# First weight slab cut to one k-tile and issued from ScalarE, normed input made inside the first projection, last output tile scaled on two engines

## Chip, core and metric

The kernel runs on one core of a Trainium2 chip. The metric is device time in microseconds of one execution. TensorE multiplies matrices, VectorE, ScalarE and GpSimd work on tiles, and SyncE (SP), ScalarE and GpSimd issue transfers (DMAs), each through a queue of its own.

## What is computed

Two residual layers on x (512 tokens x 1024 features, float32), and a final RMSNorm.

```python
u = rms_norm(x, norm_e) @ w_in_e          # even layer
q_c, kv_c, k_r, z_b, glu_a, glu_g, z_a = split(u)      # 384, 256, 32, 4 x 1024
o_b = mla(q_c, kv_c, k_r, ...) * silu(z_b)             # 16 heads of attention
o_a = conformer_conv(glu_a, glu_g, ...) * silu(z_a)    # GLU, conv of width 31, LayerNorm
x = x + concat(o_b, o_a) @ w_out_e
u = rms_norm(x, norm_o) @ w_in_o          # odd layer
z_c, xbc, dt_f, dt_b, g_b, g_c, h_d, z_d = split(u)
o_c = ssd_mixer(z_c, xbc, dt_f, dt_b, ...)             # Mamba-2, two directions
o_d = short_conv(g_b, g_c, h_d, ...) * silu(z_d)
x = x + concat(o_c, o_d) @ w_out_o
return rms_norm(x, final_norm)
```

## The kernel before

The program is unrolled, for one core. Each engine runs its own list of instructions in order. A planner sets these lists when the program is built: it goes by the order in which the program was written, and lets a later instruction go first where it expects an earlier one to be still waiting. Semaphores hold each instruction until its inputs are there.

**Products in three parts.** Every large product is done in float32 quality by splitting each operand into a rounded part (hi) and a residual (lo): hi x hi, lo x hi and hi x lo, three matmuls per k-tile of 128. For a weight slab, ScalarE casts the raw slab to hi (L91) and VectorE or GpSimd subtracts to get lo (L96). For channel slabs of the odd layer (`BY_DMA`) ScalarE writes the negative (L93) and a transfer issued by GpSimd adds the raw slab to it (L94).

**Weights.** `Weights` holds the list of all slabs in the order of use. `_prepare` issues the next slab's transfer on SP's queue and emits its split; `fetch(n)` prepares until n slabs are ready; `next` hands one out and keeps one (three for channel slabs) prepared ahead. There are two landing buffers (w_raw) and three pairs of hi and lo. In the odd layer a counter `i` gives every third channel slab an extra landing buffer and every fourth an extra pair. `i` also deals the residuals of the output projections to VectorE or GpSimd in turn.

**The start.** SP's queue loads the gains ne, then the eight tiles xt[k] (128 features x 512 tokens), with the first three slabs between them (`W.fetch` at k = 1, 4, 7) and a fourth behind them, then the constants kc, the token-major x_t (4 x 512 KB) and small parameters. Each xt[k] is multiplied by the gain and split into xg_hi (ScalarE, L266) and xg_lo (VectorE, L267). From x_t, eight squares on ScalarE (L398) and a chain of small VectorE instructions (`rsqrt`) give r4, the reciprocal root mean square of each token.

**The first projection** (qkv, 672 columns) runs in two halves b of 336 columns. A half takes eight k-tiles of weights in slabs of 2, 3 and 3 (first half) and 3, 3 and 2; in each slab `mm_tm` goes over four token tiles, and for each does the hi products and then the lo products. The first half uses the PSUM banks acc (3) and cv, the second sb and tp; ScalarE empties them with the factor r4 (L406).

**The normed input.** After both halves, `along` (L280) spreads r4 along the tokens into bank cv, and for each k VectorE scales xt[k] (L412), ScalarE casts it to xT_hi (L413), and VectorE or GpSimd subtracts to get xT_lo (L414). These feed all the channel-major products of the even layer (`mm_cm`, L325), first the two GLU tiles.

**The end.** The last projection (oo) runs in two halves of 512 columns. For each token tile t of the second half VectorE adds the residual stream (L1062), ScalarE squares (L287), a chain gives 1/rms, and the two halves are scaled by it and by the gain fg: for t < 3 the first on VectorE (L1072) and the second on ScalarE and GpSimd (L1069, L1070), for the last t both on VectorE. SP issues each store (L1073).

Of the kernel before, what the change touches and what calls it, by code (L numbers as in the profile page):

```python
# [6 lines left out]
F32 = mybir.dt.float32  # L7
# [3 lines left out]
AF = mybir.ActivationFunctionType  # L11
# [4 lines left out]
P = 128  # L16
S = 512
NT = 4
# [52 lines left out]
class Weights:  # L71


    def __init__(self, tc, pool, slabs, ahead, raw_bufs, bufs):
        self.tc, self.pool, self.slabs = tc, pool, slabs
        self.ahead, self.raw_bufs, self.bufs = ahead, raw_bufs, bufs
        self.ready, self.i, self.more = [], 0, pool

    def _prepare(self):
        nc = self.tc.nc  # L80
        key, ap, kt, n = self.slabs[self.i]
        eng = nc.vector if key in EARLY or key in ("oe", "oo") and self.i % 2 else nc.gpsimd
        self.i += 1
        more = key in BY_DMA and self.i % 3 == 0
        raw = (self.more if more else self.pool).tile([P, D], F32, name="w_raw", tag="w_raw",
                                                      bufs=1 if more else self.raw_bufs)[:, :kt * n]
        nc.sync.dma_start(raw, ap)
        more = key in BY_DMA and self.i % 4 == 0
        hi, lo = ((self.more if more else self.pool).tile([P, D], F32R, name=nm, tag=nm, bufs=1 if more else self.bufs)
                  [:, :kt * n] for nm in ("w_hi", "w_lo"))  # L90
        nc.scalar.copy(hi, raw)  # L91
        if key in BY_DMA:
            nc.scalar.mul(lo, raw, -1.0)  # L93
            nc.gpsimd.dma_start(lo, raw, accum_op=ALU.add)  # L94
        else:
            eng.tensor_tensor(lo, raw, hi.bitcast(F32), op=ALU.subtract)  # L96
        v = lambda t: t.rearrange("p (k n) -> p k n", k=kt)
        self.ready.append((key, v(hi), v(lo)))
# [27 lines left out]
def weight_slabs(A):  # L126
# [7 lines left out]

    for b in range(2):
        k0 = 0
        for kt in ((2, 3, 3), (3, 3, 2))[b]:
            out.append(("qkv", A["w_qkv"][b, :, k0:k0 + kt].rearrange("p k n -> p (k n)"), kt, 336))
            k0 += kt
    up = lambda g: out.extend((("uq", A["w_uq"][g][:, :768], 2, 384), ("uq", A["w_uq"][g][:, 768:], 1, 384),  # L140
# [37 lines left out]
def trunk(ctx, tc, A, out, dbg=None):  # L178
# [14 lines left out]
    def page(name, tag, dt=F32):  # L193
        return pg.tile([P, S], dt, name=name, tag=tag, bufs=npage[tag])
# [16 lines left out]
    def four(which):  # L211

        tags = [t for t in banks for _ in range(banks[t])]
        return tags[:4] if which == 0 else tags[4:]


    ne = cp.tile([P, KT], F32, name="ne")
    nc.sync.dma_start(ne, A["ne"])
    warm = cp.tile([P, 1], F32, name="warm")
    V.memset(warm, 0.0)  # L220
    SC.activation(warm, warm, AF.Tanh)
    W = Weights(tc, wp, weight_slabs(A), ahead=1, raw_bufs=2, bufs=3)
    kc = cp.tile([P, NKC], F32, name="kc")
    pc = cp.tile([P, NPC], F32, name="pc")
    rc = cp.tile([P, NRC], F32, name="rc")
# [149 lines left out]
    xg = [], []  # L375
    xt = []
    for k in range(KT):
        if k % 3 == 1:
            W.fetch(1 + k // 3)
        xt.append(page("xt", "att"))  # L380
        nc.sync.dma_start(xt[k], A["xT"][k])
        hi, lo = page("xg_hi", "keep", F32R), page("xg_lo", "keep", F32R)
        split_psum(hi, lo, xt[k], ne[:, k:k + 1])
        xg[0].append(hi)
        xg[1].append(lo)
# [15 lines left out]
    mean_eps(ms, ms, D)  # L401
    rsqrt(r4, ms, NT)
    qkv = [wide("qkv")[:, :672] for _ in range(NT)]
    for b in range(2):
        for t, a in mm_tm("qkv", xg, 3, 336, four(b)):
            SC.activation(qkv[t][:, b * 336:(b + 1) * 336], a[:, :336], AF.Copy, scale=r4[:, t:t + 1])  # L406

    rb = along(r4, "cv")
    xT = [], []
    xh, xl = big("xT_hi"), big("xT_lo")  # L410
    for k in range(KT):
        V.scalar_tensor_tensor(xt[k], xt[k], ne[:, k:k + 1], rb, op0=ALU.mult, op1=ALU.mult)  # L412
        SC.copy(xh[:, k], xt[k])  # L413
        (V if k % 2 else G).tensor_tensor(xl[:, k], xt[k], xh[:, k].bitcast(F32), op=ALU.subtract)  # L414
        xT[0].append(xh[:, k])
        xT[1].append(xl[:, k])
    cos, sin = (kcs(n).rearrange("p (t d) -> p t d", t=4) for n in ("cos", "sin"))

    def rope(dst, src, shape, c, s, name, G=V):
# [639 lines left out]
    for h in range(2):  # L1059
        c = slice(h * S, (h + 1) * S)  # L1060
        for t, a in mm_tm("oo", (oh, ol), 8, 512, four(h), 3 if h else 1, None if h else (6, last_group)):
            V.tensor_tensor(x1[t][:, c], a, x1[t][:, c], op=ALU.add)  # L1062
            halves_square(parts[t], x1[t], h)
            if h:
                r = rstd(part=parts[t])
                for i in range(2):
                    o = slice(i * S, (i + 1) * S)
                    if i and t < NT - 1:
                        SC.activation(x1[t][:, o], x1[t][:, o], AF.Copy, scale=r)  # L1069
                        G.tensor_tensor(x1[t][:, o], x1[t][:, o], fg[:, o], op=ALU.mult)  # L1070
                    else:
                        V.scalar_tensor_tensor(x1[t][:, o], x1[t][:, o], r, fg[:, o], op0=ALU.mult, op1=ALU.mult)  # L1072
                    nc.sync.dma_start(out[t * P:(t + 1) * P, o], x1[t][:, o])  # L1073
# [85 lines left out]
```

## Time and profile before

| | us |
|---|---|
| median of 3 runs | 958.86 (955.78 to 959.15) |
| the profiled execution | 958.48 |
| its span, first to last instruction | 956.7 |
| busy: TensorE, VectorE, ScalarE, GpSimd | 920.2, 696.0, 507.7, 310.1 |

Busy time is a sum over the span; two engines that are busy at once both count. "<-" behind an idle time names what ended it. The granted clock is the share of full speed that TensorE was given. L12 is line 12 of the kernel before.

### The profile page before, as it was taken

To read this page: it belongs to the slowest core of one execution; us is meant where nothing else is said; L and a number is where in the kernel's file an instruction comes from. 1 tells how busy PE (TensorE), PEld (TensorE's weight loads), DVE (VectorE), ACT (ScalarE), POOL (GpSimd) and SP (SyncE) were. 2 spreads that over 40 slices of the span, in tenths; PEclk is the share of its full clock that TensorE was granted. 3 is DMA by queue.
4 is the path that set the end of the run, shared out by engine and by line. 5 is a ranking of instruction groups with operands and counts; after the bars stand their busy time and mean duration, and the time that the engine had idled before them with its cause. 6 is when DMAs were issued, how large, how long until landed. Compare 5 with 4: busy or idle time off the path is not lost.

```text
span 956.7 us, 12593 instructions
## 1 busy us (share of the span) xinstructions
PE 920.2 (96%) x4528; PEld 741.1 (77%) x4528; DVE 696.0 (73%) x1292; ACT 507.7 (53%) x964; POOL 310.1 (32%) x269
## 2 busy tenths in 40 slices
PE   7899998999999999999999899999999999999996
PEld 7888686776877677888889578878786886888885
DVE  4699888999988999893163779777866886466315
ACT  6645454544554444373135487777667757444322
POOL 0142716347073443283222121121212222234222
PEclk9999999999999999999999899999999999999998
DMA  8303302212122215423347679868676776732222
GB/s 317 106 28 112 57 22 95 60 51 86 45 70 83 66 56 97 132 92 111 96 161 201 158 211 220 195 157 214 163 196 159 215 170 161 196 113 74 88 81 88
DMA packets 48373, 119.57 MB, mean 125 GB/s; under 512 B 12808, under 2 KB 14472, under 8 KB 48312
## 3 DMA queue, kind: packets, MB, share of 16 engines
q1 hardware_dynamic: 35304, 82.61, 26.7%
q0 software_dynamic: 6480, 23.60, 13.7%
q10 hardware_dynamic: 6528, 12.58, 4.4%
q8 instruction: 35, 0.57, 0.2%
q14 instruction: 26, 0.21, 0.1%
HBM read 90.85 MB, written 4.33 MB: 99 GB/s over the span
## 4 chain that ended last, share of the span: by engine, by line
PE 79%; DVE 13%; DMA 3%; ACT 3%; issue 1%; POOL 0%; SPq 0%; DVEq 0%; ACTq 0%; POOLq 0%
PE acc L325 39%; PE acc L352 10%; PE tp L352 5%; PE sb L352 5%; PE sb L536 5%; PE tp L273 5%; PE acc L573 3%; PE cv L352 3%; PE cv L945 2%; PE tp L961 1%; DMA sums_d<-sums 1%; ACT w_hi L91 1%; PE sb L273 1%; DVE w_lo L96 1%; DMA w_raw<-in_w_cm_o 1%
## 5 line engine op out<-in xcount | busy, mean ns | idle before, releaser
L325 PE MATMUL acc<-xT_hi,w_hi 128*128 128x512 f32 x616 | 249.2, 406 | 2.7 <-ACT xT_hi L413 2.7
L325 PE MATMUL acc<-xT_lo,w_hi 128*128 128x512 f32 x616 | 246.7, 401 | 0.1
L91 ACT CAST w_hi<-w_raw 128x1024 fp32r<-128x1024 f32 (+7 forms) x139 | 134.8, 971 | 200.8 <-PE acc L325 85.6
L325 PE MATMUL acc<-xT_hi,w_lo 128*128 128x512 f32 x616 | 155.1, 391 | 0.0
L96 DVE TENSOR_TENSOR w_lo<-w_raw,w_hi 128x1024 fp32r<-128x1024 f32 (+6 forms) x74 | 83.0, 1121 | 88.2 <-ACT w_hi L91 77.6
L325 PEld LDWEIGHTS acc<-xT_hi,w_hi 128*128 128x128 f32 x616 | 116.9, 190 | 27.3 <-ACT xT_hi L413 2.9
L488 DVE SCALAR_TENSOR_TENSOR cv<-u,pc,cv 128x497 f32<-128x497 f32 (+10 forms) x176 | 130.2, 740 | 10.1 <-ACT cv L477 7.7
L325 PEld LDWEIGHTS acc<-xT_lo,w_hi 128*128 128x128 f32 x616 | 116.8, 190 | 24.5 <-POOL xT_lo L414 0.8
L325 PEld LDWEIGHTS acc<-xT_hi,w_lo 128*128 128x128 f32 x616 | 115.4, 188 | 24.1
L94 POOL DMA_DIRECT2D w_lo<-w_raw x45 | 39.2, 871 | 180.5 <-ACT w_lo L93 128.2
L96 POOL TENSOR_TENSOR w_lo<-w_raw,w_hi 128x1024 fp32r<-128x1024 f32 (+1 forms) x20 | 47.7, 2387 | 112.0 <-ACT w_hi L91 104.2
L486 POOL TENSOR_TENSOR side<-side 128x510 f32<-128x510 f32 (+3 forms) x56 | 78.6, 1403 | 4.7
L491 POOL TENSOR_TENSOR u<-cs,side 128x512 f32<-128x512 f32 x8 | 11.0, 1375 | 157.1 <-issue 149.9
L540 ACT ACTIVATE p<-sb,mx 128x512 f32<-128x512 f32 x64 | 43.4, 683 | 20.8 <-DVE mx L538 20.5
L485 POOL TENSOR_SCALAR side<-u,pc 128x510 f32<-128x510 f32 (+3 forms) x56 | 50.2, 897 | 4.7
L93 ACT ACTIVATE w_lo<-w_raw 128x1024 fp32r<-128x1024 f32 x45 | 47.5, 1056 | 2.2 <-PE acc L325 2.2
L928 DVE SCALAR_TENSOR_TENSOR e<-e,nacs 128x128 f32<-128x128 f32 x96 | 30.1, 347 | 22.6 <-ACT e L927 22.5
L538 DVE TENSOR_REDUCE mx<-sb 128x1 f32<-128x512 f32 x64 | 41.7, 685 | 3.2 <-PE sb L536 2.6
L923 DVE SCALAR_TENSOR_TENSOR f<-cbm,dt,f 128x128 f32<-128x128 f32 x96 | 39.2, 444 | 5.6 <-ACT f L922 5.6
L273 PEld LDWEIGHTS tp<-kc,p 128*128 128x128 f32 x256 | 28.9, 140 | 16.1 <-ACT pt L563 10.7
L728 DVE SCALAR_TENSOR_TENSOR c<-acc,pc,c 128x510 f32<-128x510 f32 (+1 forms) x48 | 35.8, 745 | 6.3 <-ACT c L726 5.7
L536 PE MATMUL sb<-k_t,qk_hi 128*128 128x512 f32 (+1 forms) x128 | 39.5, 403 | 0.4 <-DVE k_t L264 0.4
(325 smaller groups left out, 1836.8 us busy)
## 6 DMA issues: line engine op xcount, KB each, us to landing
w_raw<-in_w_cm_o SPq DMA_DIRECT2D x45, 512.0 KB, 4.8
w_lo<-w_raw POOLq DMA_DIRECT2D x45, 512.0 KB, 5.9
w_raw<-in_w_cm_e SPq DMA_DIRECT2D x32, 512.0 KB, 3.5
e<-acs ACTq DMA_DIRECT2D x24, 512.0 KB, 6.0
w_raw<-in_w_out_e SPq DMA_DIRECT2D x16, 512.0 KB, 3.5
w_raw<-in_w_out_o SPq DMA_DIRECT2D x16, 512.0 KB, 3.3
xt<-in_xT SPq DMA_DIRECT2D x8, 256.0 KB, 5.1
x_t<-in_x SPq DMA_DIRECT2D x4, 512.0 KB, 6.3
```

Of the source, the lines that this page charges most:

```text
L91: nc.scalar.copy(hi, raw)
L93: nc.scalar.mul(lo, raw, -1.0)
L96: eng.tensor_tensor(lo, raw, hi.bitcast(F32), op=ALU.subtract)
L273: T.transpose(tp[:rows, j * P:(j + 1) * P], b, ident)
L325: T.matmul(a, l, r, start=n == 0, stop=n == 3 * kk - 1)
L352: T.matmul(accs[t][:, :n], l, r, start=k1 == 0 and c == 0, stop=end and c == len(seq) - 1)
L485: G.tensor_scalar(t[:, o], ut[:, i], wt(j), 0.0, op0=ALU.mult, op1=ALU.add)
L486: G.tensor_tensor(side[:, o], side[:, o], t[:, o], op=ALU.add)
L488: V.scalar_tensor_tensor(c[:, o], ut[:, i], wt(j), c[:, o], op0=ALU.mult, op1=ALU.add)
L536: T.matmul(s, l[:, qs], r, start=n == 0, stop=n == 2)
L538: V.tensor_reduce(mx, s, axis=AX.X, op=ALU.max, negate=True)
L540: SC.activation(p, s, AF.Exp, bias=mx, accum_out=sums[:, q:q + 1])
```

## The change

The first half's slabs become 1, 2, 3 and 2 k-tiles, one slab more. The first one's transfer is issued by ScalarE ahead of everything (`W.load`), and `_prepare` then takes it over. On SP's queue xt[0] goes first and ne second; slabs are fetched at k = 1, 3 and 5 in place of 1, 4 and 7. The making of the normed input becomes a function, `normed`, which `mm_tm` calls in the second half between its first and its second slab. In the last projection the first 512 columns of the last token tile are multiplied by fg on GpSimd in the first half, and at the end ScalarE scales them and issues their store.

```diff
+    def load(self):
+        _, ap, kt, n = self.slabs[0]
+        self.first = self.pool.tile([P, D], F32, name="w_raw", tag="w_raw", bufs=self.raw_bufs)[:, :kt * n]
+        self.tc.nc.scalar.dma_start(self.first, ap)
     def _prepare(self):
...
-        nc.sync.dma_start(raw, ap)
+        if self.first is not None:
+            raw, self.first = self.first, None
+        else:
+            raw = (self.more if more else self.pool).tile([P, D], F32, name="w_raw", tag="w_raw",
+                                                          bufs=1 if more else self.raw_bufs)[:, :kt * n]
+            nc.sync.dma_start(raw, ap)
...
-        for kt in ((2, 3, 3), (3, 3, 2))[b]:
+        for kt in ((1, 2, 3, 2), (3, 3, 2))[b]:
...
     ne = cp.tile([P, KT], F32, name="ne")
-    nc.sync.dma_start(ne, A["ne"])
+    W = Weights(tc, wp, weight_slabs(A), ahead=1, raw_bufs=2, bufs=3)
+    W.load()
...
-        if k % 3 == 1:
-            W.fetch(1 + k // 3)
+        if k in (1, 3, 5):
+            W.fetch(1 + k // 2)
         xt.append(page("xt", "att"))
         nc.sync.dma_start(xt[k], A["xT"][k])
+        if k == 0:
+            nc.sync.dma_start(ne, A["ne"])
...
-    for b in range(2):
-        for t, a in mm_tm("qkv", xg, 3, 336, four(b)):
-            SC.activation(qkv[t][:, b * 336:(b + 1) * 336], a[:, :336], AF.Copy, scale=r4[:, t:t + 1])
-
-    rb = along(r4, "cv")
     xT = [], []
     xh, xl = big("xT_hi"), big("xT_lo")
-    for k in range(KT):
-        V.scalar_tensor_tensor(xt[k], xt[k], ne[:, k:k + 1], rb, op0=ALU.mult, op1=ALU.mult)
-        SC.copy(xh[:, k], xt[k])
-        (V if k % 2 else G).tensor_tensor(xl[:, k], xt[k], xh[:, k].bitcast(F32), op=ALU.subtract)
-        xT[0].append(xh[:, k])
-        xT[1].append(xl[:, k])
+
+    def normed():
+
+        rb = along(r4, "cv")
+        for k in range(KT):
+            V.scalar_tensor_tensor(xt[k], xt[k], ne[:, k:k + 1], rb, op0=ALU.mult, op1=ALU.mult)
+            SC.copy(xh[:, k], xt[k])
+            (V if k % 2 else G).tensor_tensor(xl[:, k], xt[k], xh[:, k].bitcast(F32), op=ALU.subtract)
+            xT[0].append(xh[:, k])
+            xT[1].append(xl[:, k])
+
+    for b in range(2):
+        for t, a in mm_tm("qkv", xg, 4 - b, 336, four(b), 1, (1, normed) if b else None):
+            SC.activation(qkv[t][:, b * 336:(b + 1) * 336], a[:, :336], AF.Copy, scale=r4[:, t:t + 1])
...
             halves_square(parts[t], x1[t], h)
+            if h == 0 and t == NT - 1:
+                G.tensor_tensor(x1[t][:, c], x1[t][:, c], fg[:, c], op=ALU.mult)
             if h:
                 r = rstd(part=parts[t])
                 for i in range(2):
                     o = slice(i * S, (i + 1) * S)
+                    if t == NT - 1 and i == 0:
+                        SC.activation(x1[t][:, o], x1[t][:, o], AF.Copy, scale=r)
+                        nc.scalar.dma_start(out[t * P:(t + 1) * P, o], x1[t][:, o])
+                        continue
```

## Rows read from the trace of the kernel before

**Rows 1.** The page's busy times (us, share of the span, instructions), and from the list of TensorE's waits over the whole span: who waited for whom, us in total, how often, the longest.

```profile
PE 920.2 (96%) x4528; PEld 741.1 (77%) x4528; DVE 696.0 (73%) x1292; ACT 507.7 (53%) x964; POOL 310.1 (32%) x269
...
PE acc L352 <- ACT w_hi L91: 6.0, 1, 6.0
...
PE acc L325 <- ACT xT_hi L413: 2.7, 1, 2.7
```

**Rows 2.** Windows of 2 us: stretch, its length, busy us and instructions of TensorE, its weight loads, VectorE, ScalarE and GpSimd, then granted clock, share of the DMA engines, GB/s.

```profile
4.00:6.00 2.00, 0.05 (x1) 0.05 (x1) 0.82 (x2) 1.47 (x2) 0.00 (x0) 1.00 0.96 324
...
40.00:42.00 2.00, 0.00 (x0) 0.00 (x0) 2.00 (x3) 1.94 (x8) 0.00 (x0) 1.00 0.03 12
42.00:44.00 2.00, 1.40 (x4) 0.64 (x4) 2.00 (x4) 2.00 (x6) 1.32 (x2) 0.74 0.61 197
44.00:46.00 2.00, 2.00 (x5) 1.61 (x6) 2.00 (x4) 1.73 (x6) 1.72 (x2) 0.50 0.00 0
```

**Rows 3.** The timeline of the first 11 us: start, us, engine, line, instruction. SPq is an issue on SP's queue.

```profile
1.18 0.42 SPq L381 DMA_DIRECT2D xt<-in_xT  x1
...
4.04 0.72 ACT L266 ACTIVATE xg_hi<-xt,ne 128x512 fp32r<-128x512 f32 x1 [1.81 <-DMA xt<-in_xT]
...
5.15 0.75 ACT L91 CAST w_hi<-w_raw 128x672 fp32r<-128x672 f32 x1 [0.38 <-DMA w_raw<-in_w_qkv]
5.93 0.86 DVE L96 TENSOR_TENSOR w_lo<-w_raw,w_hi 128x672 fp32r<-128x672 f32 x1 [0.39 <-ACT w_hi L91]
...
5.95 0.65 PE L352 MATMUL acc<-w_hi,xg_hi 128*128 128x336 f32 x1 [5.95 <-ACT w_hi L91]
...
7.08 0.93 PE L352 MATMUL acc<-w_hi,xg_hi 128*128 128x336 f32 x2 [0.20 <-ACT xg_hi L266]
...
10.33 0.48 PE L352 MATMUL acc<-w_hi,xg_lo 128*128 128x336 f32 x1
...
10.61 0.48 PE L352 MATMUL acc<-w_hi,xg_hi 128*128 128x336 f32 x1
```

**Rows 4.** The timeline of ScalarE, VectorE and TensorE between 15 and 27 us: cast of the second half's first slab, the first square, cast of its second slab; start of the rsqrt chain and the residual behind it; the first two matmuls of the second half (bank sb).

```profile
15.11 1.04 ACT L91 CAST w_hi<-w_raw 128x1008 fp32r<-128x1008 f32 x1 [1.16 <-DMA w_raw<-in_w_qkv]
17.46 0.63 ACT L398 ACTIVATE junk<-x_t 128x512 bf16<-128x512 f32 x1 [1.32 <-DMA x_t<-in_x]
...
23.61 1.03 ACT L91 CAST w_hi<-w_raw 128x1008 fp32r<-128x1008 f32 x1
...
23.51 0.16 DVE L400 TENSOR_TENSOR ss<-ss 128x4 f32<-128x4 f32 x1 [6.12 <-ACT junk L398]
...
25.62 1.21 DVE L96 TENSOR_TENSOR w_lo<-w_raw,w_hi 128x1008 fp32r<-128x1008 f32 x1
...
23.97 0.31 PE L352 MATMUL sb<-w_hi,xg_hi 128*128 128x336 f32 x1
24.12 0.31 PE L352 MATMUL sb<-w_hi,xg_lo 128*128 128x336 f32 x1
```

**Rows 5.** The timeline of TensorE and VectorE between 38 and 49 us: the broadcast of r4, the first GLU matmuls and the ones from which their pace is even; VectorE's first scalings and its last subtraction.

```profile
38.75 1.05 PE L280 MATMUL cv<-kc,r 128*128 128x128 f32 x8
42.50 1.28 PE L325 MATMUL acc<-xT_hi,w_hi 128*128 128x512 f32 x3 [2.70 <-ACT xT_hi L413]
...
46.50 0.39 PE L325 MATMUL acc<-xT_lo,w_hi 128*128 128x512 f32 x1
46.73 0.39 PE L325 MATMUL acc<-xT_hi,w_hi 128*128 128x512 f32 x1
...
40.98 2.72 DVE L412 SCALAR_TENSOR_TENSOR xt<-xt,ne,cv 128x512 f32<-128x512 f32 x4
...
47.97 0.68 DVE L414 TENSOR_TENSOR xT_lo<-xt,xT_hi 128x512 fp32r<-128x512 f32 x1
```

**Rows 6.** The timeline of the end: a scaling on ScalarE of the third tile, the two on VectorE of the last, and their stores on SP's queue.

```profile
948.00 0.73 ACT L1069 ACTIVATE x<-x,rstd 128x512 f32<-128x512 f32 x1 [1.92 <-DVE rstd L255]
...
952.05 1.42 DVE L1072 SCALAR_TENSOR_TENSOR x<-x,rstd,gain 128x512 f32<-128x512 f32 x2
952.83 0.99 SPq L1073 DMA_DIRECT2D out<-x  x2
```

**Rows 7.** The start of the odd layer, in the timeline: GpSimd's issue of the first channel slab's accumulate, ScalarE's cast of a later slab and the exponential of the dt chain, TensorE's transpose of that chain's result. Then the page's transfers: line, queue, number, size, median us from issue to landing.

```profile
511.35 1.04 POOL L94 DMA_DIRECT2D w_lo<-w_raw  x1 [1.52 <-issue]
...
522.12 1.05 ACT L91 CAST w_hi<-w_raw 128x1024 fp32r<-128x1024 f32 x1 [3.86 <-DMA w_raw<-in_w_cm_o]
...
524.41 0.35 ACT L804 ACTIVATE d<-d 128x192 f32<-128x192 f32 x1
...
533.73 0.60 PE L273 MATMUL tp<-kc,d 128*24 128x128 f32 x4 [4.30 <-DVE d L817]
...
w_raw<-in_w_cm_o SPq DMA_DIRECT2D x45, 512.0 KB, 4.8
w_lo<-w_raw POOLq DMA_DIRECT2D x45, 512.0 KB, 5.9
w_raw<-in_w_cm_e SPq DMA_DIRECT2D x32, 512.0 KB, 3.5
```

**Rows 8.** The timeline where the even layer's output projection reaches the Conformer's operands: VectorE's residuals of the second and third of them, and TensorE's first matmul on the first.

```profile
422.17 4.23 DVE L368 TENSOR_TENSOR o_lo<-oT,o_hi 128x512 fp32r<-128x512 f32 x2
...
429.61 0.39 PE L352 MATMUL acc<-w_hi,o_hi 128*128 128x512 f32 x1
```

More of the change, by code (lines that the diff above doesn't have):

```diff
@@ L77, in __init__ @@
         self.ready, self.i, self.more = [], 0, pool
+        self.first = None
+    def load(self):
+        _, ap, kt, n = self.slabs[0]
+        self.first = self.pool.tile([P, D], F32, name="w_raw", tag="w_raw", bufs=self.raw_bufs)[:, :kt * n]
+        self.tc.nc.scalar.dma_start(self.first, ap)
     def _prepare(self):
@@ L84, in _prepare @@
         more = key in BY_DMA and self.i % 3 == 0
-        raw = (self.more if more else self.pool).tile([P, D], F32, name="w_raw", tag="w_raw",
-                                                      bufs=1 if more else self.raw_bufs)[:, :kt * n]
-        nc.sync.dma_start(raw, ap)
+        if self.first is not None:
[4 more added lines that the diff above has]
+            nc.sync.dma_start(raw, ap)
         more = key in BY_DMA and self.i % 4 == 0
@@ L221, in trunk @@
     SC.activation(warm, warm, AF.Tanh)
-    W = Weights(tc, wp, weight_slabs(A), ahead=1, raw_bufs=2, bufs=3)
     kc = cp.tile([P, NKC], F32, name="kc")
```

## Prediction

> **What bounds the kernel now.** I read the shares first: TensorE is busy for 96% of the span, VectorE for 73% [rows 1]. What TensorE waits for is therefore what a change can win, and the list of its waits is short: 6.0 us before the first matmul and one wait of 2.7 us on the cast of the normed input (xT_hi, L413) head it [rows 1]. Then the windows around that second wait: no matmul in 40 to 42 us, and after it a granted clock of 0.74, then 0.50 of full speed (the 1.2 GHz level) until some 46 us [rows 2]. So the wait costs more than its 2.7 us. Next the timeline of the start [rows 3], of the middle of the first projection [rows 4] and of its end [rows 5], then the last microseconds [rows 6] and the stage where the odd layer begins [rows 7]. All sums are made against the profiled execution, 958.48 us (span 956.7 and 1.8 around it), which is 0.4 us below the median of 958.86.
>
> **The start: smaller first slab, other queue, other order.** Before, TensorE starts at 5.95 us, when the cast of the 672-wide slab ends; it issues two matmuls and goes on at 7.08, at 0.28 us each (10.33 to 10.61) [rows 3]; that is the 1.2 GHz level for 336 columns, though the granted clock reads 1.00 there [rows 2]. xt[0] is used 2.86 us after its issue (1.18 to 4.04). Now it is issued where ne stood, 0.44 us earlier, beside a 168 KB slab, so it should be there at 3.6 to 4.0; ne, now behind it in SP's queue, is small and lands with it. ScalarE then needs 0.72 for xg_hi and 0.47 for the 336-wide cast (0.75 for 672 and 1.03 for 1008 [rows 3, 4], 0.28 less per k-tile), and the first matmul comes at 4.8 to 5.2; the residual (0.86 for 672, 1.21 for 1008, so 0.51) lets it run on from about 5.9. At 8.7 us twelve matmuls are done in place of eight: a lead of 4 x 0.28 = 1.1 us. It is between 0.6 (same four at 0.15, if the clock rises no earlier) and 1.5.
>
> The DMA engines are 0.96 busy between 4 and 6 us [rows 2], so a second issuing queue finds little room. The Trainium skill says why this speaks against the queue ("DMA: Bandwidth & Descriptors", "Issuing engines are not separate DMA queues"): transfers issued by different engines run on the same 16 DMA engines, and another issuer saves only the time of issuing. By that rule the queue itself is worth one SP issue, 0.42 us [rows 3], and the best case for the start below would be 0.4 and not 1.0, the sum staying as it is.
>
> **Where that lead goes.** The first fetch prepares four slabs. Before, these hold 2+3+3+3 k-tiles, so the fourth is already the first slab of the second half; its cast runs from 15.11 us, long before TensorE needs it at 23.97 [rows 4]. Now they hold 1+2+3+2, all of the first half. The second half's first slab is fetched only when the loop reaches the last slab of the first, behind kc, x, pc and rc on SP; its cast stands behind the eight squares on ScalarE and its residual behind the rsqrt chain on VectorE, just as the next slab's did before (cast at 23.61 after the squares, residual at 25.62 after the chain [rows 4]). Three k-tiles fewer ahead of x_t are 0.5 MB, 1.5 us at 324 GB/s [rows 2]; with the 0.4 of the earlier start the squares begin at 15.6 instead of 17.46 and take 6.05 (17.46 to 23.51), so they end at 21.6. The cast then ends at 22.7, the chain (2.1) at 23.75, the residual at 24.95. TensorE wants that residual after six matmuls of the first token tile. Before, that was at 23.97 + 6 x 0.15 = 24.9. It is no earlier now: **the lead of 1.1 us is waited away, and I count 0** for the start. Bounds: +1.0 if the residual is put ahead of the chain (22.7 + 1.2 = 23.9), -1.9 if x lands no earlier than before.
>
> **normed() inside the second half.** Moved: four broadcast matmuls (1.05 us for eight instructions), eight VectorE scalings, eight ScalarE casts, four subtractions each on VectorE and GpSimd; nothing is added, and no DMA moves with it. Before, TensorE ends the broadcast at 39.80, idles to 42.50, and starts nine matmuls by 46 us and the tenth by 46.50, where the 0.23 us pace begins [rows 2, 5]. Ten at 0.23 take 2.3 of these 4.0 us. The loss is 2.70 + 1.7 = **4.4 us**. Now the broadcast stands behind the second half's first slab, at 29.6; it needs r4 (23.75) and the cv bank (emptied by about 26), so it does not wait. VectorE's twelve instructions took from 40.98 to 48.65, 7.7 us, and would run from 30.7 to 38.4, GpSimd's four beside them. TensorE still has 60 matmuls of 0.154 us (9.2 us) and reaches the first GLU product at 39.8, where the broadcast ended before, and goes on at full pace. The cover is these 9.2 us; without it the 4.4 are paid as before. Queued behind VectorE's twelve are the later weight residuals: that of the first GLU slab is wanted only 16 x 0.23 = 3.7 us after 39.8, which leaves time.
>
> The one that could be late is the last qkv slab. Its landing buffer is freed at 24.95; a 512 KB slab takes 3.5 to 4.8 us to land [rows 7], its cast 0.75, so its residual can start at 29.2 to 30.5, just ahead of the twelve (30.7). I take that it does.
>
> **The tail.** The last tile's two scalings take 1.42 us on VectorE, and SP issues the two stores from 952.83 to 953.82, 0.33 each [rows 6]. The second scaling and store go to ScalarE (0.73 for the same shape), so both stores are issued at about 952.83: **0.65 us** saved (0 if ScalarE's store is slow to issue, 0.99 at most). The GpSimd product that replaces its gain runs some 40 us earlier and is waited for by nobody.
>
> **The shifted slab count.** One slab more shifts the counter that deals out VectorE or GpSimd residuals for the output projections, and, in the odd layer, which slab gets the extra landing buffer (every third) or extra pair (every fourth). At the odd layer's start ScalarE waits 3.86 us for a slab (cast at 522.12); the exponential of the dt chain is queued behind it (524.41), and TensorE waits 4.30 us for that chain (533.73) [rows 7]. That slab's buffer is held until the accumulate issued at 511.35 has landed (5.9 us: 517.2, and 4.8 more give 522). With the shift the first C slab has the extra pair and need not wait for TensorE to free one. GpSimd idled for 1.52 us before that issue, so it can come **1.5 us** earlier, and the chain with it. Bounds: 0, and all of the 4.3.
>
> **Sum.** 0 + 4.4 + 0.65 + 1.5 = 6.55; 958.5 - 6.55 = 952.0 us. TensorE has work for 96% of the span, so what it saves early should reach the end. The bounds give 947.5 (4.3 at the odd layer, 1.0 at the start, 0.99 in the tail, and 0.3 less if only nine matmuls were started by 46.5) to 955.4 (-1.9 at the start, 0 for the shift).
>
> **Rivals.**
> *The last qkv slab is late.* If its residual falls behind the twelve, it ends at 38.4 + 0.9 = 39.3, while TensorE wants it at 30.7 + 5.5 + 0.6 = 36.8: 2.5 us of the 4.4 return, and without the odd layer's 1.5 that is 956. For it: the margin is 0.2 to 1.5 us. Against: VectorE takes what is ready, and nothing else is at 30.
> *The gain is caught later.* VectorE is the second busiest; the Conformer's operands leave it at 426.40, and TensorE takes them at 429.61 [rows 8], 3.2 us of slack against 4.4 of gain. If VectorE came no earlier, this and its like in the eight head pairs could leave the tail alone: 957.8. Against: VectorE's twelve move into time in which it idled, so it is earlier too.
> *Slower: the extra landing buffer at the wrong slabs.* A slab holds its buffer for 4.8 + 1.05 + 1.05 + 5.9 = 12.8 us; two buffers carry one per 6.4 us, TensorE eats one per 24 x 0.23 = 5.5. Each channel slab whose run of five has lost its third buffer costs 0.9 us. The kernel gets slower by 0.5% from some eleven such slabs of the 45 (5.05 + 4.8 = 9.9 us); fourteen give 966. For it: ScalarE's 3.86 us wait is of this kind. Against: the waits of TensorE name no channel slab.
>
> **How the numbers follow.** Half a per cent, 4.8 us, is what a measurement of this kernel tells from no change. The forecast has 0.62, of which 0.58 lie beyond 4.8 us; the late slab 0.14 and the gain caught later 0.12, both within; the wrong buffers 0.12, of which 0.09 are slower. The range 947.5 to 957.8 leaves out the slower case and a small part below.
>
> **What would show it.** First matmul near 5.0 us; a wait of about 1 us on w_lo near 24; the broadcast near 30 us; no wait on L413 and a granted clock of 1.00 through 40 to 48; the first GLU matmul near 39.8 but at 0.23 us; the last stores issued together 0.65 us earlier. Wrong it would be by a wait on the last qkv residual near 37 us, on the Conformer's operands near 425, or on w_hi or w_lo in the odd layer.

## The result and the profile after

The changed kernel takes 961.56 us (median of 10 runs, 957.37 to 969.88) beside 958.68 us (10 runs) of the kernel before: ratio 1.0043, 95% interval 1.0024 to 1.0062. The ratio is worked out from all runs; the two medians alone lie 2.9 us apart. The changed kernel is thus 2 to 6 us slower, at the middle of the interval 4.1 us, which is less than the half per cent set as the bound of a change. The forecast was 952.0 us with 947.5 to 957.8 as its range: wrong, and on the other side. Two executions of the experiments, 1139.35 us at a granted clock of 0.85 (e8_both) and 1531.18 us at 0.557 (e11_order), are left out of every comparison. The profiled execution after took 964.18 us, span 962.4, against 958.48 and 956.7 [rows 1].

The page's busy line and the list of TensorE's waits after:

```profile
PE 922.1 (96%) x4528; PEld 742.1 (77%) x4528; DVE 702.8 (73%) x1292; ACT 508.0 (53%) x966; POOL 311.9 (32%) x270
...
PE acc L362 <- ACT xg_hi L276: 5.4, 1, 5.4
...
PE tp L283 <- DVE d L832: 2.9, 1, 2.9
PE tp L283 <- DVE qkv L456: 2.4, 1, 2.4
...
PE sb L290 <- DVE rs L265: 2.1, 1, 2.1
...
PE sb L362 <- ACT w_hi L101: 1.2, 1, 1.2
PE sb L362 <- DVE w_lo L106: 0.8, 1, 0.8
```

The wait of 2.7 us on xT_hi is gone, as forecast, and the wait on d (4.3 before [rows 7]) is shorter. But four waits are new: on w_hi and w_lo of a qkv slab, on qkv, and on rs of the LayerNorm. The timeline shows the first two, and what became of the broadcast and of the first GLU product:

```profile
17.54 0.63 ACT L410 ACTIVATE junk<-x_t 128x512 bf16<-128x512 f32 x1 [2.54 <-DMA x_t<-in_x]
...
23.53 1.03 ACT L101 CAST w_hi<-w_raw 128x1008 fp32r<-128x1008 f32 x1
24.62 0.42 PE L362 MATMUL sb<-w_hi,xg_hi 128*128 128x336 f32 x1 [1.19 <-ACT w_hi L101]
25.68 1.21 DVE L106 TENSOR_TENSOR w_lo<-w_raw,w_hi 128x1008 fp32r<-128x1008 f32 x1
26.94 0.73 PE L362 MATMUL sb<-w_lo,xg_hi 128*128 128x336 f32 x3 [0.82 <-DVE w_lo L106]
...
31.36 1.05 PE L290 MATMUL cv<-kc,r 128*128 128x128 f32 x8
41.47 0.40 PE L335 MATMUL acc<-xT_hi,w_hi 128*128 128x512 f32 x1
...
49.07 1.30 PE L283 MATMUL tp<-kc,qkv 128*128 128x128 f32 x5 [2.40 <-DVE qkv L456]
```

The squares start no earlier than before (17.46 [rows 4]), so the second half's first slab is late, and TensorE waits 2.0 us for it (1.19 for its cast, 0.82 for its residual). Windows around the GLU products answer to [rows 2]:

```profile
40.00:42.00 2.00, 2.00 (x14) 1.91 (x13) 2.00 (x3) 2.00 (x5) 1.35 (x1) 1.00 0.00 0
42.00:44.00 2.00, 2.00 (x10) 1.63 (x9) 2.00 (x3) 1.97 (x7) 0.33 (x1) 1.00 0.00 0
44.00:46.00 2.00, 2.00 (x10) 1.67 (x9) 2.00 (x12) 1.91 (x7) 0.00 (x0) 1.00 0.70 238
46.00:48.00 2.00, 0.67 (x3) 0.21 (x2) 1.93 (x19) 1.32 (x4) 0.00 (x0) 1.00 0.63 203
48.00:50.00 2.00, 0.93 (x5) 0.96 (x6) 1.90 (x9) 1.53 (x5) 0.00 (x0) 0.70 0.21 84
50.00:52.00 2.00, 2.00 (x8) 1.71 (x7) 1.24 (x3) 1.12 (x3) 0.00 (x0) 0.50 0.03 8
```

The granted clock is 1.00 where it was 0.50 before, but a hole opens behind it: TensorE works for only 1.60 of the 4 us from 46 to 50, and the clock is 0.50 in 50 to 52 us. The new wait on rs, at 406 us, is the next large loss:

```profile
403.87 0.17 DVE L264 TENSOR_SCALAR rs_t<-rs_t 128x4 f32<-128x4 f32 x1
403.92 2.34 POOL L106 TENSOR_TENSOR w_lo<-w_raw,w_hi 128x1024 fp32r<-128x1024 f32 x1 [13.47 <-PE acc L335]
404.07 2.21 DVE L265 TENSOR_TENSOR rs<-rs_t,rs_w 128x4 f32<-128x4 f32 x1
...
406.33 1.55 PE L290 MATMUL sb<-kc,rs 128*128 128x128 f32 x9 [2.10 <-DVE rs L265]
```

An instruction of 4 columns takes 2.21 us instead of 0.16: it ends when GpSimd ends the subtraction of a weight residual that the shifted count dealt to it (406.28 and 406.26). A low clock follows. Windows of 20 us of the kernel before, then of the changed one:

```profile
400.00:420.00 20.00, 19.96 (x96) 16.67 (x96) 18.66 (x26) 13.34 (x19) 10.49 (x7) 1.00 0.21 65
```

```profile
400.00:420.00 20.00, 17.90 (x83) 14.79 (x83) 17.16 (x34) 9.97 (x14) 6.00 (x4) 0.91 0.15 53
```

**Where each kernel stands.** The table is worked out from the traces: the time of the n-th matmul in the kernel before, and how much later (+) or earlier (-) it starts in the others, in us. Columns: start (75), second half of qkv (175), GLU (200 to 400, at 210 behind the ten matmuls that were slow before), head pairs (1100, 1300), LayerNorm (1900 to 2000), start of the odd layer (2500 to 2600), odd layer to its end.

```
n               75    175    200    210    300    400   1100   1300   1900   2000   2500   2600   3100   3300   4500
before        20.7   36.1   42.5   46.7   64.6   83.1  229.5  270.8  395.1  415.1  522.7  552.0  654.5  693.8  942.1
after         -0.7   +1.5   -1.0   -2.9   +1.5   +1.1   +1.6   +3.1   +3.6   +7.2   +7.2   +4.3   +5.0   +5.7   +5.6
e1_tail       -0.9   -0.9   -0.9   -0.6   +0.2   +0.2   -0.2   -0.6   -0.7   -0.7   -0.7   +1.4   +1.4   +0.2   +0.3
e2_normed     -0.7   -1.0   -3.6   -5.5   -3.3   -4.0   -4.7   -2.1   -3.3   -3.3   -3.3   -1.6   -1.6   -2.7   -2.5
e3_start      -1.0   +0.7   +0.7   +0.5   +1.2   +1.2   -0.6   -0.8   -0.3   +3.2   +3.2   +1.9   +2.7   +5.3   +5.2
e4_deal       -0.8   +1.0   -1.6   -3.5   +1.3   +0.9   +0.2   +1.3   +1.3   +1.3   +1.3   +2.5   +2.5   +3.0   +3.1
e5_early      -1.1   -1.4   -4.0   -5.9   -3.2   -2.3   -1.8   -2.2   -0.6   -0.7   -0.7   +1.3   +1.3   +0.0   +0.3
e6_slabs      -0.0   -0.4   -2.9   -4.9   -2.3   -3.0   -3.3   -1.4   -2.0   -2.0   -2.0   -0.6   -0.6   +0.3   +0.9
e7_parity     -1.4   +0.0   -2.5   -4.4   +0.2   -0.3   -1.5   -0.5   -0.6   -0.6   -0.6   +2.2   +2.8   +4.6   +4.6
e8_both       -0.1   -0.4   -2.9   -4.9   -2.6   -3.5   -3.0   -0.1   +0.0   +0.1   +0.0   -1.1   -0.3   +2.0   +2.5
e9_order      -0.3   -0.6   -3.1   -5.1   -3.2   -3.9   -2.9   -0.7   -0.5   -0.5   -0.5   -1.1   -1.1   -0.5   -0.5
e10_order     -1.2   -1.5   -4.1   -6.0   -3.9   -4.5   -4.5   -2.2   -3.0   -3.0   -3.0   -2.1   -2.0   -3.2   -3.2
e11_order     -1.0   +1.2   -1.4   -3.3   -0.5   -1.2   -1.3   +0.5   +1.1   +4.6   +4.6   +0.2   +0.9   +1.2   +1.2
e12_light     -1.0   -1.0   -1.0   -2.1   -1.4   -1.3   +5.3   +7.5   +8.5   +8.6   +8.6  +10.6  +10.6   +9.6  +10.2
e13_light     -1.0   -1.4   -3.9   -5.8   -3.6   -3.5   +1.3   +2.9   +4.1   +4.1   +4.1   +5.0   +4.9   +3.7   +4.0
```

It has to be read with care: the row e1_tail is a kernel with the same instructions as before up to the tail, and yet it stands 0.9 us earlier at 75 and 2.1 us are lost at the odd layer's start. So a single execution tells some 1 us at the start and 2 us at the odd layer; the comparison of many runs decides there. Nor does a traced execution lie at its kernel's median: 964.18 us beside 961.56 (after), 963.16 beside 959.57 (e7_parity), 959.79 beside 964.95 (e11_order). What the traces repeat is firmer. The 3.5 to 3.6 us between 1900 and 2000 matmuls are lost in all three kernels that keep the shifted dealing (after, e3_start, e11_order), and no more than 0.1 in the eleven others.

### The profile page after: what moved, and what is told of

It reads as the page before. It is cut to its first block, busy times and chain, and to the rows that moved or that the text cites. A ratio compares the mean times of both kernels' runs of the same rounds, so it can differ in the third digit from the quotient of the medians.

```text
span 962.4 us, 12609 instructions
## 1 busy us (share of the span) xinstructions
PE 922.1 (96%) x4528; PEld 742.1 (77%) x4528; DVE 702.8 (73%) x1292; ACT 508.0 (53%) x966; POOL 311.9 (32%) x270
## 4 chain that ended last, share of the span: by engine, by line
PE 70%; DVE 15%; DMA 5%; ACT 4%; issue 4%; POOL 1%; SPq 0%; ACTq 0%; POOLq 0%; DVEq 0%
PE acc L335 35%; PE acc L362 7%; PE tp L283 5%; PE sb L362 4%; PE tp L362 4%; PE sb L551 4%; PE acc L588 3%; PE cv L362 2%; DVE cv L503 2%; DVE w_lo L106 2%; PE cv L960 2%; DMA w_raw<-in_w_cm_e 2%; PE tp L976 1%; ACT w_hi L101 1%; PE sb L283 1%
## 5 line engine op out<-in xcount | busy, mean ns | idle before, releaser
L106 DVE TENSOR_TENSOR w_lo<-w_raw,w_hi 128x1024 fp32r<-128x1024 f32 (+7 forms) x75 | 90.3, 1204 | 82.1 <-ACT w_hi L101 73.3
L501 POOL TENSOR_TENSOR side<-side 128x510 f32<-128x510 f32 (+3 forms) x56 | 75.5, 1349 | 4.7
L938 DVE SCALAR_TENSOR_TENSOR f<-cbm,dt,f 128x128 f32<-128x128 f32 x96 | 41.4, 468 | 5.6 <-ACT f L937 5.6
L588 PE MATMUL acc<-pt,v_tm 128*64 128x512 f32 x128 | 38.4, 608 | 1.8 <-DVE pt L578 1.8
```

What stands on the lines that cost most here:

```text
L501: G.tensor_tensor(side[:, o], side[:, o], t[:, o], op=ALU.add)
L588: T.matmul(o[j * HD:(j + 1) * HD], v_tm[:, k, (h0 + j) * HD:(h0 + j + 1) * HD], pt, start=k == 0, stop=k == NT - 1, skip_group_check=True)
```

## The experiments

**The tail alone (e1_tail).** The kernel before with

```diff
+            if h == 0 and t == NT - 1:
+                G.tensor_tensor(x1[t][:, c], x1[t][:, c], fg[:, c], op=ALU.mult)
...
+                    if t == NT - 1 and i == 0:
+                        SC.activation(x1[t][:, o], x1[t][:, o], AF.Copy, scale=r)
+                        nc.scalar.dma_start(out[t * P:(t + 1) * P, o], x1[t][:, o])
+                        continue
```

> The kernel before with the tail's part of the change alone: the last tile's first half scaled and stored by ScalarE, its gain on GpSimd earlier. Theory A (the forecast's step): both last stores are issued at the time of the first, and the kernel is 0.65 us faster. Theory B (after the profile of the changed kernel): both stores are issued together but share the same DMA engines, so that they land about 0.8 us later after their issue than before (2.85 against 2.06 us), and from the last 1/rms to the end nothing is won: within 0.3 us of the kernel before.

Measured: ratio 1.0000 (0.9983 to 1.0017). The last 1/rms and the two last stores of this run:

```profile
952.13 0.16 DVE L255 TENSOR_TENSOR rstd<-rs_t,rs_w 128x1 f32<-128x1 f32 x1
953.07 0.40 ACTq L1072 DMA_DIRECT2D out<-x  x1
953.10 0.33 SPq L1079 DMA_DIRECT2D out<-x  x1
```

From the start of that instruction to the end of the span (957.0) it is 4.87 us, before 4.84 (951.86 to 956.7 [rows 6]). Both stores are issued within 0.03 us of each other, as forecast, and nothing is won. In the changed kernel the store issued by ScalarE lands 2.85 us after its issue, where the last one before took 2.06. The trace of the kernel before shows why nothing could be won: between 954.0 and 955.0 us its DMA engines show a busy share of 1.02 and 1.03, so the two stores, issued 0.33 us each from 952.83 on, already fill them. With both issued together the share is 1.00 and 1.02 between 954.0 and 955.0. The Trainium skill ("DMA: Bandwidth & Descriptors", "Issuing engines are not separate DMA queues") says that transfers run on the same 16 DMA engines whichever engine issues them, and that a second issuer saves only the time of issuing; the trace agrees. Theory B.

**normed() alone (e2_normed).** The kernel before, with the broadcast, scalings, casts and subtractions in a function that the second half calls:

```diff
+        for t, a in mm_tm("qkv", xg, 3, 336, four(b), 1, (1, normed) if b else None):
```

> The kernel before with normed() inside the second half alone; first slab, queues, slab count and tail as before. Theory A (the forecast's step): TensorE meets the GLU products at the full clock and with no wait on L413's counterpart, and 4.4 us are kept to the end: ratio near 0.9955. Theory B: the wait on the normed input goes, but TensorE then meets the transposes of qkv before VectorE and ScalarE have delivered qkv, waits some 2.4 us there and loses the clock behind it, so that no more than 1 us is kept: ratio 0.999 to 1.001.

Measured: 0.9989 (0.9968 to 1.0010), 1.1 us with an interval of 2 on either side. At the 210th matmul the lead is 5.5 us, 4.4 more than at the 192nd (1.1): the forecast's step is there in full, as it is in the changed kernel (from +1.5 to -2.9). Some 15 matmuls later TensorE waits at the transposes of qkv:

```profile
46.55 1.01 PE L273 MATMUL tp<-kc,qkv 128*128 128x128 f32 x6 [1.75 <-ACT junk L440]
```

That is 1.75 us of the 4.4; the granted clock stayed at 1.00 here. A lead of 3.3 to 4.7 us remains up to 1100 matmuls. Another 2.6 go between 1100 and 1300, and 1.7 at the odd layer's start, which is no more than e1_tail lost there with the old instructions. Theory B, with the later loss still open.

**The start alone, with the shifted count (e3_start).** The changed kernel with

```diff
-        for t, a in mm_tm("qkv", xg, 4 - b, 336, four(b), 1, (1, normed) if b else None):
+        for t, a in mm_tm("qkv", xg, 4 - b, 336, four(b)):
```

the normed input behind the projection and the tail as before.

> The kernel before with the start alone (four slabs of 1, 2, 3, 2 k-tiles, ScalarE's queue, new order on SP), and with it the slab count shifted by one; the normed input made after the projection, the tail as before. Theory A (the forecast): 0 for the start, 1.5 us won at the odd layer, ratio near 0.998. Theory B: x_t lands no earlier, the second half's first slab is late by about 2 us, the LayerNorm's small chain on VectorE is held by GpSimd's residual of an output-projection slab (3.5 us), and the odd layer's start gives back 2.9: 2 to 3 us slower, ratio near 1.0025.

Measured: 1.0055 (1.0031 to 1.0079), 5 us slower, more than expected. The late slab (+1.7 from 75 to 175), the wait on rs (+3.5 from 1900 to 2000) and the gain at the odd layer's start (-1.3) are all there; a wait of 2.0 us on c (L742) near 686 us with a granted clock of 0.91 in 680 to 700 adds 2.6.

**The count brought back (e4_deal).** In the changed kernel:

```diff
-        eng = nc.vector if key in EARLY or key in ("oe", "oo") and self.i % 2 else nc.gpsimd
+        eng = nc.vector if key in EARLY or key in ("oe", "oo") and (self.i - 1) % 2 else nc.gpsimd
...
-        more = key in BY_DMA and self.i % 3 == 0
+        more = key in BY_DMA and (self.i - 1) % 3 == 0
```

and the same for `% 4`.

> The changed kernel, with the count that deals out the residuals and the extra buffers brought back by one, so that every slab behind the first projection is treated as in the kernel before. Theory A (the forecast: the shift is worth 1.5 us): slower than the changed kernel by 1.5 us or more, ratio to the kernel before near 1.006. Theory B: the LayerNorm's small chain near 404 us is undisturbed again (3.5 us won), while the wait on d at the odd layer's start is back at 4.3 us (2.9 lost): about the changed kernel's time, ratio 1.002 to 1.005, with TensorE's wait on rs near 406 gone.

Measured: 1.0019 (1.0001 to 1.0037), faster than the changed kernel by 0.24% or 2.3 us, with an interval of 2.5 on either side. The wait on rs is gone, the wait on d is back at 4.7 us. Theory A's ratio of 1.006 lies outside the interval: the shift of the count, which I had counted as a gain, is none. Theory B. That it costs isn't clear of the noise in this pair of kernels alone.

**The second half's first slab early (e5_early).** The kernel of e4_deal with

```diff
-    W.fetch(4)
+    W.fetch(5)
```

> As the run that brought the count back by one, but five slabs are fetched ahead of kc and x_t in place of four, so that the second half's first slab is cast before the squares, as in the kernel before. Theory A (the late slab costs what TensorE waits at it near 24 us, and by pushing everything behind it also makes VectorE late for the transposes of qkv): no wait on w_hi or w_lo at 24 to 27 us, the lead of 0.7 us kept up to 125 matmuls, and with the wait on qkv gone or shorter the kernel is 2 to 4.5 us faster than that run: ratio to the kernel before 0.997 to 1.000. Theory B (the wait on qkv near 49 us is due to the order of the work alone): the 2 us come back at the transposes, ratio near 1.002 as without it.

Measured: 0.9990 (0.9971 to 1.0010), 2.8 us faster than e4_deal, with an interval of 2.6 on either side. The cast of that slab (first line; the second line is the next slab's) now stands ahead of the squares, which begin at 17.54:

```profile
16.33 1.04 ACT L101 CAST w_hi<-w_raw 128x1008 fp32r<-128x1008 f32 x1 [2.18 <-DMA w_raw<-in_w_qkv]
...
24.98 1.04 ACT L101 CAST w_hi<-w_raw 128x1008 fp32r<-128x1008 f32 x1 [1.43 <-DVE rs_w L262]
```

No wait on w_hi or w_lo is left (from 75 to 175 matmuls -0.3 instead of +1.8), and the longest wait on qkv is 1.4 us instead of 2.4. Theory A.

**Three slabs again (e6_slabs).** The changed kernel with

```diff
-        for kt in ((1, 2, 3, 2), (3, 3, 2))[b]:
+        for kt in ((2, 3, 3), (3, 3, 2))[b]:
...
-        for t, a in mm_tm("qkv", xg, 4 - b, 336, four(b), 1, (1, normed) if b else None):
+        for t, a in mm_tm("qkv", xg, 3, 336, four(b), 1, (1, normed) if b else None):
```

> The changed kernel with the first half in three slabs of 2, 3 and 3 k-tiles again: ScalarE still issues the first one, xt[0] still goes ahead of ne, normed() and the tail stay. So the slab count is that of the kernel before, and the fourth fetch is the second half's first slab. Theory A (what went wrong at the start is the fourth slab of the first half): no wait near 24 us, no wait on rs near 406, and the time of normed() alone or a little less: ratio 0.996 to 0.999. Theory B (ScalarE's queue and the new order delay x_t by themselves): the squares end later than 23.5 us and the ratio stays at 1.002 or more.

Measured: 0.9979 (0.9959 to 0.9998), the lowest ratio of all, though e2_normed and e5_early lie within its interval: 2 us ahead of the kernel before and 6 ahead of the changed one, with intervals of 1.9 and 2.6. No wait on w_hi, w_lo or rs is left. Theory A: the fourth slab of the first half was the fault. It brings both the late slab and the shifted count, and this run doesn't part the two; e5_early, with four slabs, is no slower than the kernel before. With the old 672-wide slab, issued from ScalarE, TensorE starts at 6.29 us, no earlier than before (5.95 [rows 3], and 5.75 to 6.41 in the other traces of the old start): the queue and the new order on SP won nothing together.

**The parity alone (e7_parity).** The changed kernel, with only the first of the three lines of e4_deal.

> The changed kernel with the dealing of the output projections' residuals to VectorE and GpSimd as in the kernel before; the phase of the odd layer's extra buffers stays shifted by one. Theory A: GpSimd's residual no longer runs beside the LayerNorm's small chain, TensorE's wait on rs near 406 (2.1 us) and the low clock behind it go, and the kernel is 3 to 3.5 us faster than the changed kernel: ratio 1.000 to 1.001; the wait on d stays near 3 us. Theory B (the stall near 406 is a matter of chance and not of who does that residual): no difference from the changed kernel, ratio near 1.004.

Measured: 1.0016 (0.9998 to 1.0034), 2.6 us faster than the changed kernel, with an interval of 2.5 on either side. The same chain with nothing beside it on GpSimd:

```profile
399.22 0.17 DVE L264 TENSOR_SCALAR rs_t<-rs_t 128x4 f32<-128x4 f32 x1
399.42 0.16 DVE L265 TENSOR_TENSOR rs<-rs_t,rs_w 128x4 f32<-128x4 f32 x1
...
399.64 2.05 PE L290 MATMUL sb<-kc,rs 128*128 128x128 f32 x16
```

Theory A, with 2.6 instead of 3 to 3.5 us. The wait on d stays at 2.8 us, and yet the traced execution loses 2.8 us between 2500 and 2600 matmuls, with a granted clock of 0.79 in 520 to 560 us (0.96 in the changed kernel). That execution is 3.6 us above the median of this run.

**normed() and the odd layer's extra buffers (e8_both).** The kernel of e2_normed with

```diff
-        more = key in BY_DMA and self.i % 3 == 0
+        more = key in BY_DMA and (self.i + 1) % 3 == 0
```

and the same for `% 4`.

> normed() inside the second half, and the odd layer's extra buffers shifted by one; start, tail and the dealing of the output projections' residuals as in the kernel before. Theory A (both parts keep what they win when nothing else moves with them): 1 to 2.5 us for normed() and 1.3 to 2 us for a wait on d of 3 us in place of 4.3 to 5.7: ratio 0.995 to 0.997. Theory B (the odd layer's start is limited by something other than the extra pair): as normed() alone, ratio near 0.999, with a wait on d of 4 us or more.

Measured: 0.9990 (0.9966 to 1.0015), as e2_normed. The wait on d fell from 5.0 to 3.2 us, so theory A's mechanism is there, but not its gain. GpSimd issues the first channel slab's accumulate at 510.42, as its own subtraction ends (508.41 and 2.06 us); in e2_normed it idled for 1.52 us there, as before [rows 7]. Windows of e2_normed, then of e8_both:

```profile
520.00:560.00 40.00, 35.02 (x145) 25.89 (x144) 26.89 (x55) 20.13 (x31) 5.02 (x6) 0.87 0.76 188
680.00:700.00 20.00, 20.00 (x110) 17.13 (x109) 14.26 (x32) 14.33 (x28) 3.58 (x4) 1.00 0.83 197
```

```profile
520.00:560.00 40.00, 36.77 (x157) 27.62 (x156) 26.70 (x55) 21.27 (x31) 5.14 (x6) 0.91 0.79 187
680.00:700.00 20.00, 18.21 (x93) 15.58 (x92) 15.76 (x33) 15.28 (x29) 3.88 (x4) 0.91 0.60 152
```

TensorE works 1.75 us more at the odd layer's start, and 1.79 us less between 680 and 700, where it waits 2.0 us on c. Whether the shift causes that second wait isn't shown: e6_slabs, unshifted, has 2.1 us there too.

**The transposes of qkv behind the GLU products (e9_order, e10_order, e11_order).** In e6_slabs, in e2_normed and in the changed kernel the first GLU pair, and the function `glu` with it, is written ahead of the work on qkv:

```diff
+    u = [glu()]
     cos, sin = (kcs(n).rearrange("p (t d) -> p t d", t=4) for n in ("cos", "sin"))
...
-    u = [glu(), glu()]
+    u.append(glu())
```

> The kernel with the old three slabs, the new queue and order, normed() and the new tail, and in the program the first pair of GLU products written ahead of the work on qkv, so that TensorE has all 48 of their matmuls before the transposes of qkv. Theory A (the rest of normed()'s gain went into the wait on qkv): no wait on qkv or its squares near 47 us, 1.8 us less than without the new order in the program, and most of it kept: ratio near 0.996. Theory B (later stages take back whatever TensorE wins here, by waits on pt and q_tm in the head pairs and on d in the odd layer): the lead at 250 matmuls is larger, the time is the same: ratio 0.997 to 0.999.

> normed() alone (start, tail and count of the kernel before) with the first pair of GLU products written ahead of the work on qkv. Theory A: the wait of 1.8 us on qkv goes and the whole 4.4 us of the forecast's step stand at 300 matmuls and at the end: ratio near 0.9955 to 0.997. Theory B: 4.4 us at 300 matmuls, but no more than about 1 us at the end, as without it: ratio near 0.999.

> The changed kernel itself, with the first pair of GLU products written ahead of the work on qkv. Theory A (of the changed kernel's loss some 4 us arise at the wait on qkv and in the low clock behind it): no wait on qkv near 49 us, granted clock 1.00 from 40 to 60 us, the late slab (2 us) and the wait on rs near 406 still there: ratio near 1.000. Theory B (the late slab makes VectorE late for whatever comes): another wait on VectorE takes the place of the one on qkv, ratio near 1.004.

Measured: 1.0006 (0.9985 to 1.0027), 1.0005 (0.9978 to 1.0031) and 1.0056 (1.0031 to 1.0081): nothing is won in any. The wait on qkv is gone, and another on the same chain of VectorE stands behind it, in e10_order:

```profile
54.08 0.66 PE L273 MATMUL tp<-kc,qkv 128*128 128x128 f32 x4 [1.82 <-DVE cT_lo L267]
```

(1.7 us in e9_order, 2.5 in e11_order). In the table e2_normed and e10_order meet again at 1100 matmuls, and lose 2.6 and 2.3 us up to 1300. Theory B in all three by what the traces show, though the times lie 1 to 2 us above what it expects.

**A lighter VectorE (e12_light, e13_light).** In the kernel before and in e2_normed:

```diff
-        for j, (o, i) in taps.items():
+        for j, (o, i) in list(taps.items())[8:]:
```

> The kernel before, with 8 of the 22 taps that VectorE adds to each of the eight tiles of the convolution of width 31 left out (the output lacks them): 64 instructions of 0.74 us, 47 us less for VectorE in the head pairs. It is the base for the next run. If VectorE sets the pace of the head pairs, it is itself faster by the 7 us that TensorE waits there (ratio near 0.993); if TensorE does, by less than 3 us.

> normed() alone, with the same 8 taps left out as in the run before, to which it is compared. Theory A (a VectorE that is busy for 90% of the head pairs takes back what TensorE wins ahead of them): with the lighter VectorE the lead at 400 matmuls (about 4 us against its base) is still 3.5 us or more at 2500, and the ratio to its base is 0.996 to 0.997. Theory B (the loss in the head pairs is no matter of VectorE's load, or comes later, at the odd layer's start): the lead shrinks by 1.5 us or more between 1100 and 1300 matmuls as without it, and the ratio to its base is 0.998 or more.

Measured: 1.0074 (1.0044 to 1.0103) and 1.0052 (1.0030 to 1.0074). The base got 7 us slower for 47 us less work on VectorE, against both of its expectations. In the traces 6.6 us arise between 400 and 1100 matmuls, 6.3 of them between 400 and 420. There the order of the instructions is another one: GpSimd is busy for 9.40 of the 10 us from 80 to 90 (0.00 before), and a residual that runs beside it stands ahead of what TensorE wants:

```profile
82.40 1.45 POOL L486 TENSOR_TENSOR side<-side 128x510 f32<-128x510 f32 x1
82.65 2.28 DVE L96 TENSOR_TENSOR w_lo<-w_raw,w_hi 128x1024 fp32r<-128x1024 f32 x1
...
84.85 0.67 DVE L264 TENSOR_TENSOR k_t<-acc,k_t 64x512 fp32r<-64x512 f32 x1
...
85.58 0.80 PE L536 MATMUL sb<-k_t,qk_hi 96*128 96x512 f32 x1 [3.13 <-DVE k_t L264]
```

The wait is 3.13 us, and the granted clock is 0.75 in 80 to 90 us (1.00 before). Against this base the lead of e13_light is 2.2 us at 400 matmuls, 4.6 at 1300 and 4.5 at 2500: it doesn't shrink in the head pairs, as theory A has it. But the two orders differ as much as the two loads, and the ratio of the two (1.0052 to 1.0074, 0.9978) lies between what the theories expect, with an interval of 3.5 us on either side. So it isn't shown that VectorE's load takes the gain.

A part of what e2_normed loses between 1100 and 1300 matmuls can be seen in its trace. There pt, which TensorE wants for the products of the heads, stands behind a weight residual that itself takes 2.15 us in place of 1.22:

```profile
253.00 1.28 POOL L494 TENSOR_TENSOR u<-cs,side 128x512 f32<-128x512 f32 x1 [22.46 <-issue]
253.21 2.15 DVE L96 TENSOR_TENSOR w_lo<-w_raw,w_hi 128x1024 fp32r<-128x1024 f32 x1 [1.36 <-ACT cs L493]
255.28 0.68 DVE L566 COPY pt<-tp 128x512 f32<-128x512 f32 x1
256.02 0.66 PE L273 MATMUL tp<-kc,p 128*128 128x128 f32 x4 [0.64 <-DVE pt L566]
```

The lead falls by 1.1 us around this wait, from 4.3 to 3.2; where the other 1.5 us go isn't shown. In the kernel before the hand-over of a convolution tile from ScalarE to GpSimd (cs) comes at 262.30, here at 252.29, so GpSimd works beside other instructions of VectorE.

## Why the prediction was wrong

**The sum by measured parts.** Of the forecast's 6.55 us, normed()'s 4.4 came at their place and were mostly lost again, and the 0.65 of the tail and the 1.5 of the odd layer never reached the time. Two costs that the sum had at nothing came instead: the late slab and the dealing of residuals. In numbers: normed() -1.1 us (e2_normed), the tail 0, the late slab +2.8 (e4_deal against e5_early), the dealing of the residuals +2.6 (the changed kernel against e7_parity): +4.3, and 4.1 was measured. Each has an interval of 1.6 to 2.6 us on either side, which makes some 4 us for the sum, so that the close agreement is partly luck. It holds for another kernel too: e3_start 5.4 by it and 5.3 measured. What is clear of the noise is the two together: e6_slabs, without late slab and shifted count, is 6.1 us faster than the changed kernel, with an interval of 2.6. How they share it rests on the waits in the traces and on two pairs of kernels that are barely clear of the noise.

**The start.** The step "with the 0.4 of the earlier start the squares begin at 15.6" failed: they begin at 17.54. I had worked it out from bytes at a constant rate. SP's queue is held until a landing buffer is free for the fourth slab, which it issues at 10.32 us (11.30 before), and x_t behind it is issued at 11.16 (12.15): 1.0 earlier, not 1.9; and the transfers of x_t then take 7.6 us to land in the median, where they took 6.3. Between 6 and 12 us the DMA engines moved 306, 357 and 335 GB/s in the changed kernel, 350, 400 and 392 in the one before. So the bound that I gave for "x lands no earlier", -1.9, was the case; the waits are 1.19 and 0.82. The lead of 1.1 us isn't there either: the first matmul comes at 5.41 us, not at 4.8 to 5.2, and at 75 matmuls kernels with the old start stand between 0 and -1.2, those with four slabs between -0.7 and -1.4. The rule of the Trainium skill ("DMA: Bandwidth & Descriptors", "Issuing engines are not separate DMA queues"), that a second issuer saves only the time of issuing, fits what e6_slabs shows (6.29 us beside 5.95).

**normed().** The mechanism was right, and so was the 4.4 us at its own place (-1.1 to -5.5 in e2_normed): no wait on the counterpart of L413, the broadcast at 31.36, the GLU products at 0.23 us each and a granted clock of 1.00 from 40 to 46 us. The step that failed is "goes on at full pace": I checked the residuals that queue behind VectorE's twelve instructions, and not the chain of qkv that queues there as well, and whose transposes the planner had put among the GLU matmuls. That wait was 1.75 us in e2_normed and 2.40 in the changed kernel, where the late slab had made everything later and the clock was lost as well. What was left, 2.6 us, was 1.1 at the end by the many runs. The sentence "what it saves early should reach the end" was the larger mistake, and the rival that the gain is caught later, with 0.12, the better account of this part, though not at the place that it named: no wait on the Conformer's operands near 425 us appears, and in e2_normed 2.6 us go in the head pairs. e10_order removed the wait on qkv and still won nothing.

**The shifted count.** Of the 1.5 us for the extra pair the mechanism was right (the wait on d is 2.7 to 3.2 us with the shift, 4.3 to 5.7 without, and the 1.52 us ahead of the accumulate are gone), but e8_both shows no gain in time, with an interval of 2.4 us. The extra pair and the extra landing buffer shift together in every run, so which of them does it isn't shown. What failed outright is that I named the dealing of the output projections' residuals and gave it no price. Its cost is the wait on rs: 2.10 us in the trace and 3.5 to 3.6 with the low clock behind it, 2.6 by many runs (interval 2.5). The Trainium skill would have told where to look ("SBUF — State Buffer", "Who interferes with whom"): a VectorE instruction with two inputs in SBUF and a GpSimd instruction that reads SBUF exclude each other, and the one that comes second waits for the whole of the other. The trace agrees: L265 ends at 406.28, GpSimd's subtraction at 406.26.

**The tail.** Its bound of 0 came true, but not for the reason given with it: ScalarE's store is issued in time. The term of 0.65 took the issue of a store for its end, while the DMA engines were full with both.

**The rivals.** The slower one had the wrong mechanism: no channel slab is waited for. The late last qkv slab didn't come about either; it was the first slab of that half, for which I had counted only the lead as "waited away", and no cost.

**A better version.** e6_slabs keeps normed(), the new queue and the new tail, and leaves the slabs as they were; with 0.9979 (0.9959 to 0.9998) it beats both, by 2 and 6 us. The win over the kernel before is at the edge of the noise, and normed() alone (0.9989) explains half of it.

## What to carry to other kernels

When an edit moves the place at which TensorE waits, follow the whole list of the engine that it waited for: the next instruction of that list that TensorE needs is the next wait. An edit that changes a count which deals out work (to engines, to buffers) changes it for every later user, so price each of them, above all a long GpSimd instruction that lands beside a chain of tiny VectorE ones. Where an order is planned when the program is built, a few us won early can be lost again in a later stage whose order they changed, and one execution's trace doesn't tell that from its own spread of 1 to 2 us.

## What the runs showed of the hardware

A VectorE instruction on 128x4 elements took 2.21 us instead of 0.16 beside one GpSimd subtraction of 2.34 us, and a residual of 1.22 us took 2.15 and 2.28 when GpSimd had begun on its own instruction 0.2 us earlier; both times it ended 1.08 us after GpSimd did. After TensorE's wait of 2.40 us on qkv the granted clock was 0.50 in 50 to 52 us, in e4_deal as in the changed kernel; after the waits of 1.75 us in e2_normed and 1.4 in e5_early it stayed at 1.00. And 47 us less work on VectorE made a kernel 7 us slower, while GpSimd and VectorE took another order.
